# Two-layer hybrid trunk on one core: the first layer's modulation weights in couples, its norm's squares summed on VectorE

## The chip, the cores and the metric

The kernel runs on one core of a Trainium2 chip. The metric is the device time of one execution in microseconds; several executions are timed and their median is given. Engines are called by the profile's names: PE (TensorE's matmuls), PEld (its weight loads), DVE (VectorE), ACT (ScalarE), POOL (GpSimd) and SP (SyncE, which here only issues DMAs).

## The reference, cut to what matters

A trunk of two layers over 256 context tokens and 256 latent tokens of width 1024. Each layer mixes tokens (RWKV-7 heads beside gated linear attention) and then applies a feed-forward part, a dense SwiGLU in the first layer and eight experts in the second. Only the beginning of the first layer matters here:

```python
mod_x = jnp.split((silu_c @ ada_w[i] + ada_b[i])[:, None, :], 6, axis=-1)
mod_c = jnp.split((silu_cc @ ada_w[i] + ada_b[i])[None, None, :], 6, axis=-1)
hx = modulate(rmsnorm(x, norm_mix_pre[i]), mod_x[0], mod_x[1])
hc = modulate(rmsnorm(h_ctx, norm_mix_pre[i]), mod_c[0], mod_c[1])
# rmsnorm(x, g) = x * rsqrt(mean(x * x) + eps) * g;  modulate(h, shift, scale) = h * (1 + scale) + shift
pc, px = hc @ w_in, hx @ w_in
```

So every value of `h` needs the norm over all 1024 features of its token, and its feature's shift (the first sixth of the modulation) and scale (the second sixth). The first projection needs all of `h`.

## The kernel before, in words

Activations lie with features on the 128 partitions: 8 blocks (k = 0 to 7) of 128 features by 512 tokens. Weights stream from memory in pieces of 1 MB (128 partitions by 2048) through a ring of three `raw` buffers; SP issues the loads in the order of the list `pieces` (class `Stream`, line 267), and the load of a piece waits until the matmuls of the piece three places ahead of it have read their buffer. When a piece of the projection is used, it is split in halves: `hi` is a rounded copy made by ACT (line 299) and `lo` the remainder made by DVE (line 300), and each product is three matmuls (`hh` by `hi`, `hl` by `hi`, `hh` by `lo`; line 386), where `hh` and `hl` are the rounded copy and the remainder of `h`.

The order of the work is the order in which the program text issues it: every engine has its own queue of instructions and gets them in that order. Generators interleave the streams; `staggered(gens, lag)` starts one generator every `lag` rounds and steps all live ones once a round.

The modulation of one layer is 24 pieces of 256 outputs each; pieces 0 to 3 are the shift and 4 to 7 the scale of the first norm. One piece is one generator `ada(l, i, i + 1)`: PE multiplies the conditioning by the piece in two steps of eight matmul instructions (line 408), ACT copies the resulting row to SBUF (`arow`, line 412), PE turns the row into columns (line 417), DVE adds the bias and writes `mods` (line 419). After piece 7 one DVE instruction makes `gsc`, the norm's weight times (1 + scale), for all eight blocks (line 427).

`h_first` (line 1713 and on) is the beginning of the first layer. POOL's queue loads the small constants and then the whole input `xc` (2 MB). The pieces 0 to 7 go through `staggered` with a lag of 2, and the generator `stats` stands between the third and the fourth: for each block ACT squares it (line 461) and PE adds the squares over the partitions by a matmul with ones (line 467); ahead of the last squares a tiny Ln makes ACT load its table (line 454). At the end ACT computes `rstd` with Ln and Exp (lines 474 and 475). Then `W.ahead` splits the first projection piece, and `norm_mod` makes the eight blocks: `xn` = input times `rstd` (line 494, DVE or POOL), `h` in two halves of 256 tokens on ACT (line 501), `hh` (line 517 on ACT, line 520 on DVE) and `hl` (line 521, DVE or POOL). Its loop makes block k's `h` ahead of `hh` and `hl` of block k - 1. `mixing` then starts the projection; its first two output blocks run interleaved, 48 matmuls that go through k = 0 to 7.

Of the kernel before, what the change touches and what calls it, by code (L numbers as in the profile page):

```python
# [7 lines left out]
F32 = mybir.dt.float32  # L8
# [8 lines left out]
P = 128  # L17
# [20 lines left out]
         [("rw", b) for b in (14, 12, 13, 8, 9, 10, 11, 4, 0, 5, 1, 6, 2, 7, 3)])  # L38

GLA_QKV, GLA_O, GLA_V = (5, 9), 13, 20  # L40
FGROUPS = [(0, 8), (8, 15), (15, 22)]

FFN_END = 24 + 8 + 14 + 4 + 22 + 24
# [83 lines left out]
def body(tc, nc, A):  # L127
# [10 lines left out]
    def nm(s):  # L138
        cnt[0] += 1
        return f"{s}{cnt[0]}"  # L140
# [52 lines left out]
    def bc(ap, n):  # L193

        return bass.AP(tensor=ap.tensor, offset=ap.offset, ap=[*ap.ap, [0, n]])
# [6 lines left out]
    def run(g):  # L202
        for _ in g:
            pass
# [125 lines left out]
            b = self.take()  # L330
            return (a[0], b[0]), (a[1], b[1])

    for i in range(8):
        pieces.append((A["ada"][0, i], PIECE, False))
    for i in range(14):
        pieces.append((A["win"][0, i], PIECE, True))
# [62 lines left out]
    def ada(l, i0, i1, tag="acc"):  # L399

        for i in range(i0, i1):
            yield tag
            raw = W.get()[0][0]
            pt = ps(tag)
            for kk in range(2):
                for q in range(4):
                    k = 2 * q + kk
                    mm(pt[32 * q:32 * q + 32, :256], silc[:, k, :], raw[:, k * 256:k * 256 + 256],
                       start=(kk == 0), stop=(kk == 1), tile_position=(0, 32 * q))
                yield  # L410
            row = wp.tile([P, 256], F32, tag="arow", name=nm("arow"), bufs=2)
            sc.copy(row, pt[:, :256])
            back(tag)
            yield tag
            pt = ps(tag)
            for b in range(2):
                mm(pt[:, 2 * b:2 * b + 2], row[:, b * P:b * P + P], K("sel"), start=True, stop=True)
            yield
            ve.tensor_tensor(mods[l][:, 2 * i:2 * i + 2, :], pt[:, 0:4].rearrange("p (a b) -> p a b", b=2),
                             bc(V(l, "ada_b", 2 * i, 2 * i + 2), 2), ALU.add)  # L420
            back(tag)
            if i % 4 == 3:
                c = i // 4
                m = mods[l][:, 8 * c:8 * c + 8, :]
                if c in (1, 4):
                    n = V(l, "norm_mix_pre" if c == 1 else "norm_ffn_pre")
                    ve.scalar_tensor_tensor(gsc[l][0 if c == 1 else 2], m, 1.0, bc(n, 2), ALU.add, ALU.mult)
                if c in (2, 5):
                    n = V(l, "norm_mix_post" if c == 2 else "norm_ffn_post")
                    ve.tensor_tensor(gsc[l][1 if c == 2 else 3], m, bc(n, 2), ALU.mult)  # L430
            yield True

    def staggered(gens, lag):

        live, t, todo = [], 0, list(gens)
        while live or todo:
            if todo and t % lag == 0:
                live.append(todo.pop(0))
            live = [g for g in live if steps(g, 1)]
            t += 1  # L440
# [37 lines left out]
    def stats(src, q, out, late):  # L478
        for k in range(KB):
            q.add(src[:, k, :])  # L480
            q.mm()
            yield
        for _ in range(late):
            yield
        out.append(q.r())

    def norm_mod(l, which, res, r, n0, hh, hl, tp, keep=None):

        n = T - n0
        sh = mods[l][:, 24 * which:24 * which + 8, :]  # L490
        g = gsc[l][2 * which]
        def norm(e, k):
            xn = tp.tile([P, T], F32, tag="xn" if e is ve else "pxn", name=nm("xn"), bufs=2)[:, :n]
            e.tensor_tensor(xn, res[:, k, :], r, ALU.mult)
            return xn

        def mod(k, xn):
            h = keep[:, k, :] if keep is not None else tp.tile([P, T], F32, tag="h", name=nm("h"), bufs=NH)[:, :n]
            for (a, b, m) in SEG:
                if a >= n0:  # L500
                    sc.activation(h[:, a - n0:b - n0], xn[:, a - n0:b - n0], AF.Identity, scale=g[:, k, m:m + 1],
                                  bias=sh[:, k, m:m + 1])
            return h
        if hh is None:
            for k in range(KB):
                mod(k, norm(ve, k))
                yield
            return

        hs, xs = {}, {k: norm(gp, k) for k in XN_POOL[:2]}  # L510
        for k in range(KB + 1):
            if k < KB:
                h = hs[k] = mod(k, xs.pop(k) if k in xs else norm(ve, k))
                if k == XN_POOL[0]:
                    xs.update({q: norm(gp, q) for q in XN_POOL[2:]})
                if k in HH_ACT:
                    sc.copy(hh[:, k, :n], h)  # L517
            if k > 0:
                if k - 1 not in HH_ACT:
                    ve.tensor_copy(hh[:, k - 1, :n], hs[k - 1])  # L520
                (gp if k - 1 in HL_POOL else ve).tensor_tensor(hl[:, k - 1, :n], hs[k - 1], hh[:, k - 1, :n], ALU.subtract)  # L521
                yield
# [1187 lines left out]
    with tc.manual_schedule():  # L1710
        banks(**MAIN)

        def h_first(l):
            sp = ExitStack()
            W.sp = sp.enter_context(pool("sp", "right"))
            hs = ExitStack()
            hp = hs.enter_context(pool("hp", "right"))
            hh = hp.tile([P, KB, T], F32R, name="hh0")
            hl = hp.tile([P, KB, T], F32R, name="hl0")
            with pool("ra") as ra:  # L1720
                res = ra.tile([P, KB, T], F32, name="res0")
                gp.dma_start(res, A["xc"])
                r = []
                first = [ada(l, i, i + 1) for i in range(8)]
                staggered(first[:3] + [stats(res, Squares(T, hp, "pa", "xn"), r, 3)] + first[3:], 2)
                W.ahead(W.i, 2)
                run(norm_mod(l, 0, res, r[0], 0, hh, hl, hp))

            def close():
                hs.close()  # L1730
                sp.close()
            return hh, hl, hp, close

        y, og, left = mixing(0, h_first)
        rs = ExitStack()
        rb = rs.enter_context(pool("rb", "right"))
        res = rb.tile([P, KB, T], F32, name="res")
        gp.dma_start(res, A["xc"])
        sp2 = ExitStack()
        W.sp = sp2.enter_context(pool("sp", "right"))  # L1740
        W.nhi = 4
        W.limit = 2 * FFN_END
        st = rb.tile([P, T], F32, name="st0")
        with pool("op", "right") as tp:
            r = out_proj(0, y, og, res, 0, tp, Squares(T, tp))
            ve.tensor_copy(st, r)
        left.close()
        ls = ExitStack()
        res1 = ls.enter_context(pool("ra")).tile([P, KB, T], F32, name="res1")
        with pool("fh", "right") as hp:  # L1750
            nxt = ffn(0, res, st, res1, hp)
        sp2.close()
        rs.close()

        def h_second(l):
            sp = ExitStack()
            W.sp = sp.enter_context(pool("sp", "right"))
            W.nhi = 2
            W.limit = 2 * (FFN_END + 14)
            hs = ExitStack()  # L1760
            hp = hs.enter_context(pool("hp", "right"))
            hh = hp.tile([P, KB, T], F32R, name="hh1")
            hl = hp.tile([P, KB, T], F32R, name="hl1")
            nxt.tp = hp
            W.ahead(W.i, 2)
            run(norm_mod(l, 0, res1, nxt.r(), 0, hh, hl, hp))
            gp.dma_start(A["rx"], res1[:, :, 256:512])
            ls.close()

            def close():  # L1770
                hs.close()
                sp.close()
            return hh, hl, hp, close

        y, og, left = mixing(1, h_second)
        rs = ExitStack()
        rb = rs.enter_context(pool("rb", "right"))
        res = rb.tile([P, KB, 256], F32, name="res")
        gp.dma_start(res, A["rx"])
        sp3 = ExitStack()  # L1780
        W.sp = sp3.enter_context(pool("sp", "right"))
        W.nhi = 4
        W.limit = 1 << 30
        st = rb.tile([P, 256], F32, name="st1")
        with pool("op", "right") as tp:
            r = out_proj(1, y, og, res, 256, tp, Squares(256, tp))
            ve.tensor_copy(st, r)
        left.close()
        xr = ExitStack()
        W.widen(xr.enter_context(pool("xr")), 6)  # L1790
        moe(1, res, st)
        xr.close()
        sp3.close()
        rs.close()
        psum[2].close()
# [85 lines left out]
```

## Time and profile before

| | |
|---|---|
| median of 3 executions | 2387.55 us (2386.76 to 2390.78) |
| the profiled execution's own time | 2388.32 us |
| its span in the profile | 2386.5 us |
| mean granted TensorE clock | 0.939 of full speed |
| PE busy | 2172.3 us (91%) |
| DVE busy | 1517.9 us (64%) |
| ACT busy | 1264.7 us (53%) |

The span is measured from the first to the last record of the profiled execution; its own time is 1.8 us longer. Busy shares are averages over stages with different limits: the change touches only the beginning, so that stretch is read by itself. In the timeline each line gives the start, the duration, the engine, the line of the program and what is written from what; a bracket tells how long the engine had been idle before and which instruction or load ended the wait.

### The profile page before, as it was taken

To read this page: it belongs to the slowest core of one execution; us is meant where nothing else is said; L and a number is where in the kernel's file an instruction comes from. 1 tells how busy PE (TensorE), PEld (TensorE's weight loads), DVE (VectorE), ACT (ScalarE), POOL (GpSimd) and SP (SyncE) were. 2 spreads that over 40 slices of the span, in tenths; PEclk is the share of its full clock that TensorE was granted. 3 is DMA by queue.
4 is the path that set the end of the run, shared out by engine and by line. 5 is a ranking of instruction groups with operands and counts; after the bars stand their busy time and mean duration, and the time that the engine had idled before them with its cause. 6 is when DMAs were issued, how large, how long until landed. Compare 5 with 4: busy or idle time off the path is not lost. (4 is left out here: it accounts for less than half of the span.)

```text
span 2386.5 us, 37180 instructions
## 1 busy us (share of the span) xinstructions
PE 2172.3 (91%) x14845; PEld 1718.9 (72%) x14845; DVE 1517.9 (64%) x2204; ACT 1264.7 (53%) x1861; POOL 240.9 (10%) x597
## 2 busy tenths in 40 slices
PE   6999888978699999879978887699999999999997
PEld 3777666766488888658756776578778787887875
DVE  2547555753532333365765565488998998999996
ACT  4435434544423222354554344577777777777775
POOL 1000034430200000120003451000000000000000
PEclk8989889998799999979986898899999999999998
DMA  6211354323023231212223432469998998999981
GB/s 261 85 66 59 121 179 148 101 89 124 22 76 122 70 127 66 84 67 89 76 97 111 129 106 72 179 261 345 346 351 328 342 362 332 348 346 352 364 346 69
DMA packets 110310, 430.79 MB, mean 181 GB/s; under 512 B 51584, under 2 KB 54144, under 8 KB 62000
## 3 DMA queue, kind: packets, MB, share of 16 engines
q1 hardware_dynamic: 102800, 377.53, 43.7%
q10 hardware_dynamic: 5472, 39.85, 4.8%
q0 software_dynamic: 1856, 10.95, 1.3%
q8 instruction: 118, 1.93, 0.3%
q14 instruction: 64, 0.52, 0.1%
HBM read 417.81 MB, written 10.49 MB: 179 GB/s over the span
## 5 line engine op out<-in xcount | busy, mean ns | idle before, releaser
L300 DVE TENSOR_TENSOR lo<-raw,hi 128x1024 fp32r<-128x1024 f32 (+1 forms) x668 | 797.2, 1222 | 209.1 <-ACT hi L299 196.6
L299 ACT CAST hi<-raw 128x1024 fp32r<-128x1024 f32 (+1 forms) x668 | 685.2, 1048 | 157.3 <-PE ps_acc L1586 68.2
L1586 PE MATMUL ps_acc<-hi,gh 128*128 128x512 f32 x704 | 285.1, 405 | 0.0
L1586 PE MATMUL ps_acc<-hi,gl 128*128 128x512 f32 x704 | 278.6, 396 | 0.0
L1586 PE MATMUL ps_acc<-lo,gh 128*128 128x512 f32 x704 | 278.1, 395 | 0.0
L386 PE MATMUL ps_acc<-hh,hi 128*128 128x512 f32 (+1 forms) x448 | 181.1, 404 | 12.5 <-ACT hh L517 10.6
L386 PE MATMUL ps_acc<-hl,hi 128*128 128x512 f32 (+1 forms) x448 | 172.7, 385 | 2.9 <-POOL hl L521 2.2
L386 PE MATMUL ps_acc<-hh,lo 128*128 128x512 f32 (+1 forms) x448 | 172.5, 385 | 1.5 <-DVE lo L300 1.5
L1586 PEld LDWEIGHTS ps_acc<-lo,gh 128*128 128x128 f32 x704 | 132.3, 188 | 32.1 <-DVE lo L300 0.2
L1586 PEld LDWEIGHTS ps_acc<-hi,gl 128*128 128x128 f32 x704 | 132.6, 188 | 27.0
L1586 PEld LDWEIGHTS ps_acc<-hi,gh 128*128 128x128 f32 x704 | 132.4, 188 | 27.2
L1610 PE MATMUL ps_pc<-hi,eah 128*128 128x512 f32 x352 | 139.6, 397 | 0.0
L1610 PE MATMUL ps_pc<-lo,eah 128*128 128x512 f32 x352 | 139.2, 395 | 0.0
L1610 PE MATMUL ps_pc<-hi,eal 128*128 128x512 f32 x352 | 139.2, 395 | 0.0
L386 PEld LDWEIGHTS ps_acc<-hh,hi 128*128 128x128 f32 x448 | 89.0, 199 | 36.9 <-ACT hh L517 11.6
L1400 DVE TENSOR_TENSOR s<-s,ps_pa 128x512 f32<-128x512 f32 x22 | 15.1, 687 | 141.0 <-PE ps_pa L374 141.0
L386 PEld LDWEIGHTS ps_acc<-hl,hi 128*128 128x128 f32 x448 | 88.8, 198 | 20.0 <-POOL hl L521 3.6
L386 PEld LDWEIGHTS ps_acc<-hh,lo 128*128 128x128 f32 x448 | 88.7, 198 | 18.5 <-DVE lo L300 2.8
L547 POOL TENSOR_TENSOR xn<-macc,rstd 128x256 f32<-128x256 f32 x2 | 1.8, 923 | 853.8 <-ACT rstd L475 853.8
L873 POOL TENSOR_TENSOR Tt<-Nl,Tl 64x15 f32<-64x15 f32 (+7 forms) x240 | 69.5, 290 | 153.2 <-DMA Nl<-nsc 135.8
L467 PE MATMUL ps_pc<-nsq,ones 128*128 128x512 f32 (+1 forms) x112 | 56.9, 636 | 30.2 <-ACT nsq L461 30.1
L374 PE MATMUL ps_acc<-fhh,hi 128*128 128x512 f32 x176 | 69.5, 395 | 10.3 <-ACT fhh L517 10.3
(408 smaller groups left out, 4355.5 us busy)
## 6 DMA issues: line engine op xcount, KB each, us to landing
raw<-moe SPq DMA_DIRECT2D x264, 1024.0 KB, 5.7
raw<-ada ACTq DMA_DIRECT2D x34, 1024.0 KB, 5.1
raw<-win SPq DMA_DIRECT2D x28, 1024.0 KB, 4.9
raw<-fgu SPq DMA_DIRECT2D x22, 1024.0 KB, 4.9
raw<-ada SPq DMA_DIRECT2D x14, 1024.0 KB, 5.1
raw<-fdn SPq DMA_DIRECT2D x16, 448.0 KB, 3.2
res<-xc POOLq DMA_DIRECT2D x2, 2048.0 KB, 12.4
Q<-tsc SPq DMA_DIRECT2D x32, 128.0 KB, 2.8
```

What stands on the lines that cost most here:

```text
L299: sc.copy(hi[:, :n], t[:, a * HALF:a * HALF + n])
L300: ve.tensor_tensor(lo[:, :n], t[:, a * HALF:a * HALF + n], hi[:, :n], ALU.subtract)
L374: mm(out, w[:, o:o + P], x[:, k, n0:n1], start=(n == 0 and j == 0), stop=(n == len(ks) - 1 and j == 2))
L386: mm(out, a[:, o], x[:, k, n0:T], start=(k == 0 and j == 0), stop=(k == KB - 1 and j == 2))
L467: mm(self.pt, ones, self.todo.pop(0)[:, :self.n], start=(self.made == 0), stop=(self.made == KB - 1))
L547: e.tensor_tensor(t, m[:, k, :], r, ALU.mult)
L873: gp.tensor_tensor(tmp[:, u, j], bc(Nl[:, s, t], s + 1), bcm(Tl[:, s, j], NB - 1 - s), ALU.mult)
L1400: ve.tensor_tensor(s, s, pu, ALU.mult)
L1586: mm(pg, x[:, k, :], ww, start=(k == 0 and j == 0), stop=(k == 7 and j == 2))
L1610: mm(pd[q], x[:, i * P:i * P + P], ww, start=(c == 0 and i == 0 and j == 0), stop=(c == 10 and i == 1 and j == 2))
```

## The change

The input is loaded by SP's queue in two halves ahead of all pieces. The eight modulation pieces come in the order of `FIRST`, a piece of the shift followed by the piece of the scale for the same 256 features, and `gsc` is made couple by couple. The squares are summed on DVE into two tiles, so that only those two go through PE. The blocks of `h` are made two at a time by a new `block`, the first two after the seventh piece, the others after the eighth; POOL takes no part, and `hh` is made by ACT for the first four blocks and by DVE for the rest. `W.ahead`, which splits the first projection piece, now stands behind all blocks. `norm_mod` is still used by the second layer.

```diff
+FIRST = (0, 4, 1, 5, 2, 6, 3, 7)
...
-    for i in range(8):
+    for i in FIRST:
         pieces.append((A["ada"][0, i], PIECE, False))
...
-            if i % 4 == 3:
+            if l == 0 and 4 <= i < 8:
+                ve.scalar_tensor_tensor(gsc[l][0][:, 2 * i - 8:2 * i - 6, :], mods[l][:, 2 * i:2 * i + 2, :], 1.0,
+                                        bc(V(l, "norm_mix_pre", 2 * i - 8, 2 * i - 6), 2), ALU.add, ALU.mult)
+            elif i % 4 == 3:
...
-                gp.dma_start(res, A["xc"])
-                r = []
-                first = [ada(l, i, i + 1) for i in range(8)]
-                staggered(first[:3] + [stats(res, Squares(T, hp, "pa", "xn"), r, 3)] + first[3:], 2)
+                for q in range(2):
+                    sy.dma_start(res[:, 4 * q:4 * q + 4], A["xc"][:, 4 * q:4 * q + 4])
+                g, sh = gsc[l][0], mods[l][:, 0:8, :]
+                pt = ps("pa")
+                r = hp.tile([P, T], F32, tag="rstd", name="rstd", bufs=1)
+                sq = [hp.tile([P, T], F32, tag="h", name=nm("acc"), bufs=NH) for _ in range(2)]
+
+                def squares():
+
+                    for k in range(KB):
+                        s = sq[k] if k < 2 else hp.tile([P, T], F32, tag="pxn", name=nm("nsq"), bufs=2)
+                        sc.activation(s, res[:, k, :], AF.Square)
+                        if k > 1:
+                            ve.tensor_tensor(sq[k % 2], sq[k % 2], s, ALU.add)
+                        if k % 2 == 1:
+                            yield
+                    sc.activation(tiny, eps[1e-6], AF.Ln)
+                    yield
+
+                def norm():
+                    for q in range(2):
+                        mm(pt, ones, sq[q], start=(q == 0), stop=(q == 1))
+                    sc.activation(r, pt, AF.Ln, bias=eps[1e-6], scale=1.0 / D)
+                    sc.activation(r, r, AF.Exp, scale=-0.5)
+                    yield
+
+                def block(k):
+                    xn = hp.tile([P, T], F32, tag="xn", name=nm("xn"), bufs=2)
+                    ve.tensor_tensor(xn, res[:, k, :], r, ALU.mult)
+                    h = hp.tile([P, T], F32, tag="h", name=nm("h"), bufs=NH)
+                    for (a, b, m) in SEG:
+                        sc.activation(h[:, a:b], xn[:, a:b], AF.Identity, scale=g[:, k, m:m + 1], bias=sh[:, k, m:m + 1])
+                    (sc.copy if k < 4 else ve.tensor_copy)(hh[:, k, :], h)
+                    ve.tensor_tensor(hl[:, k, :], h, hh[:, k, :], ALU.subtract)
+                    yield
+                first = [ada(l, i, i + 1) for i in FIRST]
+                staggered(first[:3] + [squares()] + first[3:4], 2)
+                staggered([first[4], norm(), first[5]], 1)
+                for a, p in ((6, 0), (7, 2), (None, 4), (None, 6)):
+                    staggered(first[a:a + 1] if a else [], 1)
+                    run(chained(block(p), block(p + 1)))
                 W.ahead(W.i, 2)
-                run(norm_mod(l, 0, res, r[0], 0, hh, hl, hp))
```

## Rows read from the trace of the kernel before

**Rows 1.** Busy time by stretch: length, each engine's busy time, granted clock, DMA share, GB/s

```profile
0.00:64.70 64.70, 42.84 (x224) 23.50 (x224) 18.57 (x42) 24.85 (x43) 12.23 (x16) 0.87 0.67 253
```

**Rows 2.** Timeline of the opening stretch, 11 to 42 us: start, duration, engine, line, operation

```profile
11.37 1.08 PE L408 MATMUL ps_acc<-raw,silc 128*32 128x256 f32 x8 [2.75 <-DMA raw<-ada]
12.38 1.01 PE L417 MATMUL ps_acc<-cst,arow 128*128 128x2 f32 x4
...
14.47 0.37 ACT L412 COPY arow<-ps_acc 128x256 f32<-128x256 f32 x1 [5.42 <-PE ps_acc L408]
...
20.58 3.78 PE L467 MATMUL ps_pa<-nsq,ones 128*128 128x512 f32 x4 [0.29 <-ACT nsq L461]
...
24.40 0.63 ACT L461 ACTIVATE nsq<-res 128x512 f32<-128x512 f32 x1 [1.08 <-PE ps_pa L467]
...
26.46 0.64 PE L408 MATMUL ps_acc<-raw,silc 128*32 128x256 f32 x8
...
27.03 1.13 PE L467 MATMUL ps_pa<-nsq,ones 128*128 128x512 f32 x2
...
29.18 1.28 ACT L454 ACT_TABLE_LOAD   x1
...
30.47 0.20 ACT L454 ACTIVATE tiny<-eps 128x1 f32<-128x1 f32 x1
...
34.84 0.61 PE L417 MATMUL ps_acc<-cst,arow 128*128 128x2 f32 x4
...
36.40 0.69 ACT L474 ACTIVATE rstd<-ps_pa,eps 128x512 f32<-128x512 f32 x1
...
38.41 0.63 ACT L475 ACTIVATE rstd<-rstd 128x512 f32<-128x512 f32 x1
...
41.83 0.16 DVE L419 TENSOR_TENSOR mods<-ps_acc,vec 128x4 f32<-128x4 f32 x1 [1.68 <-PE ps_acc L417]
```

**Rows 3.** DMA: two stretches of the stretch table, and issues with us to landing

```profile
10.00:12.50 2.50, 1.13 (x9) 0.33 (x9) 0.00 (x0) 0.00 (x0) 0.00 (x0) 1.00 1.08 450
...
25.00:27.50 2.50, 2.50 (x13) 0.83 (x12) 0.00 (x0) 1.29 (x3) 0.00 (x0) 1.00 0.07 30
...
res<-xc POOLq DMA_DIRECT2D x1, 2048.0 KB, 16.9
...
raw<-ada SPq DMA_DIRECT2D x1, 1024.0 KB, 4.8
```

**Rows 4.** Timeline of the split and the blocks, 41 to 49 us, ACT and DVE

```profile
41.12 1.99 ACT L299 CAST hi<-raw 128x1024 fp32r<-128x1024 f32 x2 [0.16 <-DMA raw<-win]
...
43.34 1.22 DVE L300 TENSOR_TENSOR lo<-raw,hi 128x1024 fp32r<-128x1024 f32 x1
...
45.20 1.09 ACT L501 ACTIVATE h<-xn,mods,gsc 128x256 f32<-128x256 f32 x2 [2.08 <-DVE xn L494]
46.32 0.62 ACT L517 CAST hh<-h 128x512 fp32r<-128x512 f32 x1
...
46.97 0.69 DVE L521 TENSOR_TENSOR hl<-h,hh 128x512 fp32r<-128x512 f32 x1 [1.21 <-ACT hh L517]
...
47.96 0.43 DVE L520 CAST hh<-h 128x512 fp32r<-128x512 f32 x1 [0.30 <-ACT h L501]
48.31 0.68 DVE L494 TENSOR_TENSOR xn<-res,rstd 128x512 f32<-128x512 f32 x1
```

**Rows 5.** Timeline of PE in the first projection, 46 to 65 us

```profile
46.99 0.80 PE L386 MATMUL ps_acc<-hh,hi 128*128 128x512 f32 x1 [5.19 <-ACT hh L517]
...
52.84 0.63 PE L386 MATMUL ps_acc<-hh,lo 128*128 128x512 f32 x1
...
58.38 0.40 PE L386 MATMUL ps_acc<-hh,hi 128*128 128x512 f32 x1
...
64.32 0.39 PE L386 MATMUL ps_acc<-hh,lo 128*128 128x512 f32 x1
```

**Rows 6.** Busy time by stretch around PE's pause, columns as in group 1

```profile
40.00:42.00 2.00, 1.30 (x12) 0.73 (x10) 0.32 (x2) 1.25 (x2) 1.61 (x2) 0.83 0.85 250
42.00:44.00 2.00, 0.00 (x0) 0.00 (x0) 1.97 (x3) 1.11 (x2) 0.00 (x0) 0.50 0.96 360
```

## The prediction, made before the changed kernel was run

> **What bounds the kernel now.** I read the stretch table first. The first 64.7 us hold everything that the diff touches, and PE is busy for 42.84 of them [rows 1]. Behind that stretch comes a chain through the projection, the scans and the experts in which each stage needs the one before it. Nothing in it is tied to absolute time, because the ring of three weight buffers can't run ahead by more than three pieces, so I take a shift of the first projection's end as a shift of the whole kernel.
>
> Then the timeline, engine by engine. In the opening stretch PE works through eight modulation pieces: two groups of eight matmuls and one turn of the row (`sel`) for each. The eight took 1.08 us at first and 0.64 us later, a turn 1.01 and then 0.61 [rows 2]. That is the lower and the upper of TensorE's two levels (1.2 and 2.4 GHz). The granted clock column reads 1.00 through those early microseconds, so there I go by durations. The squares of the input lie between, each on ACT with two `ones` matmuls behind it: four took 3.78 us at the lower level, two took 1.13 at the upper [rows 2]. ACT waited 1.08 us for PE before one of them, and PE, waiting in turn, freed buffers late: the DMA moved 450 GB/s in the stretch from 10 us and 30 GB/s in that from 25 us [rows 3]. That is the loss that the change can attack.
>
> The last modulation result lands on DVE at 41.83 us [rows 2]. Then two casts on ACT and two subtractions on DVE split the first projection piece [rows 4], and the eight blocks of `hh`/`hl` follow. There the reader is to see the order: while one block is multiplied, the block before it is split, and POOL takes some of the operations. PE starts at 46.99 us, **before** the blocks are complete, and follows them; the last of the first 48 matmuls starts at 64.32 and ends at 64.7 us [rows 5]. In this first stretch the blocks and the projection overlap almost fully. The number to beat is 64.7 us.
>
> **The change, part by part.**
>
> *Loads.* The two halves of `xc` (1 MB each) come ahead of the pieces in SP's queue, which also carries the pieces; POOL's queue loses its 2 MB. The second piece, which is the second 1 MB of that queue before, had landed by 11.4 us [rows 2]; the second half of `xc` takes its place. One more MB at 450 GB/s [rows 3] or a little less is 2.4 us, less some half microsecond that POOL's share of `xc` had cost this queue by then: the first piece lands at about 13.3 us, the next two at 15.8 and 18.2. The input comes earlier than before, where it took 16.9 us from issue [rows 3]. Each later piece waits until its buffer's former matmuls are through, plus 4.8 us for a load alone [rows 3].
>
> *Squares.* Sixteen matmul instructions become four, six additions of 128x512 come to DVE. No such addition is in the rows; the same shape's multiply took 0.68 us [rows 4] and I take 0.69 (at least the 0.43 of a copy, at most the 1.22 of half the split [rows 4]: within 4 us for all six, on DVE, idle here). ACT's row copy of the second piece ends at about 19.3, so two squares, the third piece's copy, then six squares at 0.63 to 0.69 us each end ACT's part at 26.4 us. The table for Ln costs 1.28 plus 0.20 [rows 2], and **the fourth piece's row copy is queued behind it**: 28.2 us, though its matmuls were through at 25.3. On PE the next pieces are queued behind that copy's turn.
>
> *The norm.* PE: turn 0.6, eight matmuls 0.6, two sums 2.1 (from the 1.13 row): 31.6 us. ACT: Ln 0.69, a second table load 1.28, Exp 0.63 [rows 2]: `rstd` at 34.3 us, and the fifth piece's row copy stands behind all three. The last piece's buffer is held by the fifth's second half behind the sums, so it can't land before about 37 us. Then fifth, sixth and seventh pieces follow each other on ACT and PE by 0.37 (copy), 0.6 (turn), 0.6 (second half) and some 0.1 of handing over: 1.7 us each. The seventh's modulation is on DVE at 39.5 us. Against 41.83 for the last one before, this part does win; it wins little because ACT's queue takes PE's old place.
>
> *The blocks.* They are emitted one after another: `xn` on DVE, `h` on ACT, `hh` on ACT (first four) or DVE, `hl` on DVE, and only then the next block's `xn`. DVE takes its instructions in order: at 46.97 it had stood 1.21 us for `hh` [rows 4] although the `xn` of a later block, behind it in its queue, had its inputs. So each block costs the length of its chain: 0.68 + 0.10 + 1.09 + 0.62 + 0.69 = 3.2 us with ACT's `hh`, 0.68 + 0.10 + 1.09 + 0.43 + 0.69 = 3.0 us with DVE's [rows 4], with a few hundredths for each handing over. The two-step overlap of before and POOL's help are gone. Blocks 0 and 1: 39.5 + 6.4 = 45.9. The eighth piece's row copy is behind block 1 on ACT (45.6); turn 0.6, modulation and its new small scale instruction 0.3: 46.6. That part is nearly hidden. Blocks 2 and 3 to 53.0, blocks 4 to 7 (4 x 3.03) to 65.1 us.
>
> *The split of the first projection piece* stands behind the blocks in the code. ACT's casts run beside the last `hl`, DVE's two subtractions don't: 1.22 us to 66.4 us for the first, the second by 67.6 beside PE.
>
> *The first projection* now finds everything made, but starts with all its work ahead. Two matmuls need no `lo`; 46 remain at 66.4. Between the start at 52.84 and that at 58.38 thirteen steps took 0.426 us each (lower level), from there to 64.32 twenty-six took 0.229 (upper) [rows 5]. PE will have had little to do for 20 us, as before it started here (0.00 us busy in the two microseconds from 42, granted clock 0.50) [rows 6], so I give it the same 13 slow steps: 5.6 + 33 x 0.229 = 13.1, end 79.5 us.
>
> **Sum:** 79.5 - 64.7 = +14.8 us. Against the profiled execution (2388.32 us, span 2386.5) that gives 2403.1; that execution stands 0.8 us above the median of 2387.55, so against the median 2402.4 us. The bounds: 46 matmuls all at the upper level end at 76.9 (2.6 less), all at the lower at 86.0 (6.5 more); loads 0.6 us earlier and shorter hand-overs take 1.5 off; PE's share of the pieces and norm at the lower level instead puts 5 on.
>
> *The clock in the pieces.* The granted clock was 0.83 in the two microseconds from 40 and 0.50 in those from 42, after PE had had 1.30 of 2 us to do [rows 6]; while it was kept busier, the durations stayed at the upper level. In the changed kernel PE waits for ACT between 25.3 and 28.3 us and often after. The Trainium skill, page "TensorE: Matmul & The Clock Gate", section "Part 1: The HAM clock gate", says that the half-rate state is the default and that only activity lifts it; by that, PE could be back at half rate from 28 us. My sum takes the upper level there; the other is a rival below.
>
> **The rivals.** 0.2% or 4.8 us is about what a measurement can tell from no change here.
>
> *PE stays at the lower level through the pieces.* Turns and eights cost 1.0 instead of 0.6, the two sums 3.8 instead of 2.1: the seventh modulation comes at 44.4, everything behind 5 us later: about 2407.5. For it: the gaps that ACT's queue puts into PE. Against: PE is busy without a break from about 16 to 25 us. With the projection slow as well it is 2414. This is the rule named above.
>
> *Early start.* If ACT's squares, tables and copies don't hold up the pieces, they land every 2.5 to 3 us and the seventh modulation is made at about 31. The serial blocks then end at 56.6, the first `lo` at 57.8, the projection at 68.3 (upper level) to 70.9: +3.6 to +6.2, 2391 to 2394. Against: the two table loads and three row copies that stand behind the norm in one queue.
>
> *Faster: an engine passes over an instruction that waits.* Place: DVE and ACT. Then `xn` of the next block runs while `h` of this one is made, the row copies don't wait for the norm, blocks cost DVE's own 1.4 to 1.8 us each, and with a start at 31 the last ends at about 47, the split at 48 to 49, the projection at 60.5: -4 us or a little more, 2383. It decides where `xn` of block 1 starts before `hl` of block 0 ends. The 1.21 us row speaks against it.
>
> *The change doesn't do what it says* only in one sense: the couples come, but just the first couple of blocks is made beside a piece; that is in the sum.
>
> **Chances.** The sum as it stands 0.73; the lower level through the pieces 0.16; early start 0.06, split over the bound; passing over 0.04; 0.01 for the rest. Range 2396 to 2410: it takes in the bounds on both sides and the first rival, leaves out the two lighter ends. Faster by over 0.2% 0.04, within 0.2% 0.05, slower 0.91.
>
> **What would show it.** Right: in the new timeline `xn`, `h`, `hh`, `hl` of one block follow each other without the next block's `xn` between them, some 3 us from one `xn` to the next; the fourth piece's row copy behind the Ln table load; the first projection matmul between 63 and 68 us, with `lo` behind the last `hl`; POOL empty of `xn` and `hl`; from then on the old stages shifted by one amount. Wrong: PE's first projection matmul before 55 us, blocks at under 2 us each, or a later stage that gives the shift back.

## The result and the profile after

The changed kernel took 2417.2 us (median of 4 executions, 2410.13 to 2422.58) against 2389.16 us (4 executions, 2386.76 to 2394.96): a ratio of 1.0112, 95% interval 1.0074 to 1.0150. It is slower by some 28 us where 14.8 were forecast, and outside the range that ended at 2410. Over all experiments the changed kernel ran 16 times (mean 2414.8 us, standard error 1.2) and the kernel before beside them 50 times (mean 2391.4, standard error 0.6): 23.4 us, give or take 1.4. Its three series, each against the runs of the kernel before beside it, differ in the mean by 26.8, 24.7 and 20.3 us.

The profiled execution is one of the longer ones (2422.09 us). The page's span and its first lines:

```profile
span 2420.2 us, 37169 instructions
...
PE 2180.3 (90%) x14833; PEld 1725.0 (71%) x14833; DVE 1521.9 (63%) x2216; ACT 1266.7 (52%) x1864; POOL 232.4 (10%) x590
```

Busy times moved little (PE's by 8.0 us, where the span grew by 33.7): most of the time was lost by waiting. Its timeline of the pieces and the norm answers to [rows 2] (start, duration, engine, line, operation):

```profile
14.58 1.94 PE L410 MATMUL ps_acc<-raw,silc 128*32 128x256 f32 x16 [14.58 <-DMA raw<-ada]
...
18.68 1.08 PE L410 MATMUL ps_acc<-raw,silc 128*32 128x256 f32 x8 [2.16 <-DMA raw<-ada]
...
28.95 1.28 ACT L1743 ACT_TABLE_LOAD   x1
...
30.35 0.35 ACT L414 COPY arow<-ps_acc 128x256 f32<-128x256 f32 x1
...
30.76 1.02 PE L419 MATMUL ps_acc<-cst,arow 128*128 128x2 f32 x4 [2.81 <-ACT arow L414]
...
32.71 3.78 PE L1748 MATMUL ps_pa<-acc,ones 128*128 128x512 f32 x4
...
36.43 1.31 PE L410 MATMUL ps_acc<-raw,silc 128*32 128x256 f32 x16
...
36.53 0.69 ACT L1749 ACTIVATE rstd<-ps_pa,eps 128x512 f32<-128x512 f32 x1 [5.83 <-PE ps_pa L1748]
...
39.07 0.35 ACT L414 COPY arow<-ps_acc 128x256 f32<-128x256 f32 x1
...
41.26 1.01 PE L419 MATMUL ps_acc<-cst,arow 128*128 128x2 f32 x4 [0.47 <-ACT arow L414]
...
45.73 0.16 DVE L421 TENSOR_TENSOR mods<-ps_acc,vec 128x4 f32<-128x4 f32 x1 [3.06 <-PE ps_acc L419]
```

The reader sees the two hold-ups that were forecast: the fourth piece's row copy right behind the Ln table, the fifth's behind Ln, the Exp table and Exp. And one that the sum had left to a rival: a turn takes 1.01 or 1.02 us and the two sums 3.78, so PE works at its lower level through most of the pieces.

The blocks, the split and PE's start, answering to [rows 4, 5]:

```profile
45.81 0.69 DVE L1755 TENSOR_TENSOR xn<-res,rstd 128x512 f32<-128x512 f32 x1
...
46.54 1.09 ACT L1758 ACTIVATE h<-xn,mods,gsc 128x256 f32<-128x256 f32 x2 [1.91 <-DVE xn L1755]
47.66 0.62 ACT L1759 CAST hh<-h 128x512 fp32r<-128x512 f32 x1
48.31 0.69 DVE L1760 TENSOR_TENSOR hl<-h,hh 128x512 fp32r<-128x512 f32 x1 [1.81 <-ACT hh L1759]
48.92 0.68 DVE L1755 TENSOR_TENSOR xn<-res,rstd 128x512 f32<-128x512 f32 x1
...
70.40 0.69 DVE L1760 TENSOR_TENSOR hl<-h,hh 128x512 fp32r<-128x512 f32 x1
...
70.90 0.79 PE L388 MATMUL ps_acc<-hh,hi 128*128 128x512 f32 x1 [18.18 <-ACT hi L301]
71.01 2.35 DVE L302 TENSOR_TENSOR lo<-raw,hi 128x1024 fp32r<-128x1024 f32 x2
...
72.29 0.80 PE L388 MATMUL ps_acc<-hh,lo 128*128 128x512 f32 x1 [0.17 <-DVE lo L302]
...
84.11 0.57 ACT L1271 COPY gad<-ps_acc 32x512 f32<-32x512 f32 x1
```

From one `xn` to the next are 3.11 us, with DVE and ACT waiting for each other in turn; PE stands idle for 18.18 us and then has all 48 matmuls before it. ACT's copy of `gad` is the first work behind those 48. Its start is called **the mark** below: 64.80 us before, 84.11 here.

```profile
64.80 0.57 ACT L1266 COPY gad<-ps_acc 32x512 f32<-32x512 f32 x1
```

### The profile page after: what moved, and what is told of

It reads as the page before. It is cut to its first block, busy times and chain, and to the rows that moved or that the text cites. A ratio compares the mean times of both kernels' runs of the same rounds, so it can differ in the third digit from the quotient of the medians.

```text
span 2420.2 us, 37169 instructions
## 1 busy us (share of the span) xinstructions
PE 2180.3 (90%) x14833; PEld 1725.0 (71%) x14833; DVE 1521.9 (63%) x2216; ACT 1266.7 (52%) x1864; POOL 232.4 (10%) x590
## 3 DMA queue, kind: packets, MB, share of 16 engines
q1 hardware_dynamic: 103088, 379.63, 43.5%
## 5 line engine op out<-in xcount | busy, mean ns | idle before, releaser
L388 PEld LDWEIGHTS ps_acc<-hl,hi 128*128 128x128 f32 x448 | 88.1, 197 | 17.2 <-DVE hl L526 1.3
```

What stands on the lines that cost most here:

```text
L388: mm(out, a[:, o], x[:, k, n0:T], start=(k == 0 and j == 0), stop=(k == KB - 1 and j == 2))
```

## The experiments

Theory A: the loss is that of the start-up, some 20 us at the mark, and the rest of the 28 is a spread between executions. Its main rival, B: a late start costs more again behind the mark. The parts of the start-up's loss are then taken apart one by one. Each edit is to the changed kernel unless the text says otherwise.

**The changed kernel again, twice,** unaltered.

> The changed kernel once more, unaltered. Two parts are told apart by the mark, the start of ACT's copy of gad, the first work behind the first projection's 48 matmuls (64.80 us before, 84.11 after). Theory A (only the beginning is changed; what is lost later is TensorE's granted clock falling at other moments of the scans, from run to run and in any kernel): the mark again at 83 to 85, the stretch from the mark to the end anywhere between 2322 and 2336 us, so runs from 2408 to 2423 us. Rival B (the change makes the scans slower by itself): the mark the same and the stretch behind it again near 2336, every run above 2418.

> The changed kernel a third time, for more times and a third profile. Theory A: the mark at 83 to 86; runs between 2405 and 2423 us, the mean of all runs so far (2416) minus that of the kernel before (2390) comes down to the shift of the mark, 20 to 22 us. Rival B (something behind the mark is slower by itself): the difference of the means stays at 24 us or more, and the profile's stretch behind the mark is above 2330.

The marks were 85.68 and 84.41 us, and the stretch behind the mark 2320.0 and 2326.3 us, where the first profile had 2336.1. The first ran 2407.44 to 2421.02 us, the second 2409.41 to 2416.93. So the start-up is lost every time (mean mark of the three profiles 84.73), and what follows varies by 16 us with the same program. The stretch table from the mark to the output projection of the first layer, for the kernel before, the changed kernel's first profile, and its second, in this order (length, busy times, granted clock, DMA share, GB/s):

```profile
64.80:545.40 480.60, 431.52 (x4673) 339.00 (x4673) 285.64 (x554) 215.72 (x380) 95.47 (x277) 0.94 0.33 104
```

```profile
84.10:575.20 491.10, 443.49 (x4673) 347.43 (x4673) 285.19 (x554) 215.83 (x380) 95.13 (x277) 0.91 0.32 102
```

```profile
85.70:567.30 481.60, 432.18 (x4673) 339.68 (x4673) 282.98 (x554) 215.90 (x380) 95.79 (x277) 0.94 0.33 104
```

Same number of instructions, ACT within 0.2 us; PE is busy 12 us longer where the granted clock is 0.91 instead of 0.94, and the stretch is 10 us longer. The changed kernel's second profile has the length of the kernel before. The mark of 85.68 lies just above what was expected, the stretch behind it, 2320.0, below. Runs well under 2418 us and two stretches near those of the kernel before speak against B as it was put. Theory A's number isn't met either: the means differ by 23.4 us (give or take 1.4), not 20 to 22.

**The kernel before again, twice,** as a measure of its own spread.

> The kernel before once more, for a second profile. Theory A (TensorE's clock rises and falls at other moments in every run): its mark anywhere between 60 and 65 us by when the clock rises in the first projection, all work of ACT and DVE ahead of it unmoved (blocks from 44 to 45 us on), and the stretch behind the mark between 2318 and 2332. Rival: 64.8 and 2322 again within 0.5 us.

> The kernel before against itself. Theory A: ratio 1 within 0.3%, the runs spread over 12 us or more, and the profile's mark between 60 and 65 with the stretch behind it between 2318 and 2332. Rival: runs within 3 us of each other, which would make the spread of the changed kernel its own.

Marks 63.87 and 64.54, stretches behind it 2327.3 and 2325.2 us. The second time, in 12 runs, it ran from 2387.96 to 2403.20 us, ratio to itself 0.9997 (0.9981 to 1.0013). So the spread is not the changed kernel's own, and the mean mark of three profiles before is 64.40: the start-up's shift is 84.73 - 64.40 = 20.3 us.

**The kernel before, delayed.** Does lateness alone cost more later?

```diff
                 W.ahead(W.i, 2)
+                for _ in range(29):
+                    d = hp.tile([P, T], F32, tag="xn", name=nm("late"), bufs=2)
+                    ve.tensor_tensor(d, res[:, 0, :], r[0], ALU.mult)
                 run(norm_mod(l, 0, res, r[0], 0, hh, hl, hp))
```

> The kernel before with 29 further multiplies on DVE (0.645 us apart, so 18.7 us) between the split and the blocks; nothing else is moved. Theory A: the mark at 83 to 85 and, behind it, the same spread as in the changed kernel, so 2405 to 2423 us, median about 2412. Rival B: the mark the same, but the stretch behind it as in the kernel before (2320 to 2326 us), so 2405 to 2411 us in every run.

The multiplies took less than I had set (first `h` at 62.44 instead of 45.20: 17.2 us), and the mark came only 14.4 us late, 79.18: PE reached its upper level at 69.5, five microseconds after its start at 64.2, where the kernel before needed eleven ([rows 5]). The stretch behind was 2323.7 us. The runs: 2411.02 us median (2401.11 to 2416.45), ratio 1.0086 (1.0062 to 1.0110), which is 15 to 26 us. Its lower end lies just above the delay of the mark (14.4 us, 14.8 from the mean mark of 64.40): there may be a rest of some us here too, but this doesn't tell A from B.

**Overlapping blocks.**

```diff
-                def block(k):
...
+                def blocks(k0, k1):
+                    hs = {}
+                    for k in range(k0, k1 + 1):
...
+                            ve.tensor_tensor(xn, res[:, k, :], r, ALU.mult)
+                        if k > k0:
+                            (sc.copy if k <= 4 else ve.tensor_copy)(hh[:, k - 1, :], hs[k - 1])
...
+                                sc.activation(h[:, a:b], xn[:, a:b], AF.Identity, scale=g[:, k, m:m + 1], bias=sh[:, k, m:m + 1])
+                        if k > k0:
+                            ve.tensor_tensor(hl[:, k - 1, :], hs[k - 1], hh[:, k - 1, :], ALU.subtract)
+                        yield
...
-                for a, p in ((6, 0), (7, 2), (None, 4), (None, 6)):
-                    staggered(first[a:a + 1] if a else [], 1)
-                    run(chained(block(p), block(p + 1)))
+                staggered(first[6:7], 1)
+                run(blocks(0, 2))
+                staggered(first[7:8], 1)
+                run(blocks(2, 8))
```

> The changed kernel with the blocks in two overlapping steps: the next block's xn ahead of hh and hl of this one, blocks 2 to 7 in one go. Theory (the serial chain of 3.0 to 3.2 us a block is what the blocks cost): blocks cost 1.7 to 1.8 us each, the last hl ends near 63 instead of 71, the mark comes at 76 to 77 instead of 84.1, and the time falls by 8 us. Rival (the blocks are bound by the engines' own work or by something that the trace doesn't show): the mark stays within 2 us of 84.

Its timeline of DVE late in the blocks, and the mark:

```profile
58.36 0.68 DVE L1758 TENSOR_TENSOR xn<-res,rstd 128x512 f32<-128x512 f32 x1
58.96 0.42 DVE L1760 CAST hh<-h 128x512 fp32r<-128x512 f32 x1
...
59.41 0.69 DVE L1766 TENSOR_TENSOR hl<-h,hh 128x512 fp32r<-128x512 f32 x1
60.02 0.68 DVE L1758 TENSOR_TENSOR xn<-res,rstd 128x512 f32<-128x512 f32 x1
...
76.12 0.57 ACT L1271 COPY gad<-ps_acc 32x512 f32<-32x512 f32 x1
```

Late in the blocks DVE works without a pause, 1.66 us a block instead of 2.9 to 3.1; the last `hl` starts at 62.39 instead of 70.40, the mark is at 76.12. Median 2403.58 us, ratio 1.0069 (1.0044 to 1.0095). The serial chain is shown as the blocks' price: 8 of the 20 us.

**An earlier split.**

```diff
                     staggered(first[a:a + 1] if a else [], 1)
+                    if p == 2:
+                        W.ahead(W.i, 2)
                     run(chained(block(p), block(p + 1)))
-                W.ahead(W.i, 2)
```

> The changed kernel with the split of the first projection piece moved ahead of blocks 2 to 7, so that PE can follow the blocks as before; the blocks stay serial. Theory (PE's start behind all blocks costs the length of the 48 matmuls): PE starts at about 54 instead of 71, its blocks end 2.4 us later (73), the mark comes at about 76 instead of 84.1, 8 us less. Rival (PE, following a slow chain, stays at the lower clock level, and the 48 matmuls take the time that the overlap saves): the mark at 82 to 86.

```profile
53.08 2.36 DVE L302 TENSOR_TENSOR lo<-raw,hi 128x1024 fp32r<-128x1024 f32 x2
54.36 0.80 PE L388 MATMUL ps_acc<-hh,lo 128*128 128x512 f32 x1 [0.44 <-DVE lo L302]
...
60.98 0.50 PE L388 MATMUL ps_acc<-hh,hi 128*128 128x512 f32 x1 [0.95 <-ACT hh L1759]
...
74.97 0.57 ACT L1271 COPY gad<-ps_acc 32x512 f32<-32x512 f32 x1
```

Mark 74.97, 2404.61 us median, ratio 1.0067 (1.0041 to 1.0094). PE follows the serial blocks with waits of 0.2 to 1 us and still gains 10 us: where PE starts is worth about as much as the blocks' chain. The two edits were not run together by themselves, so that 8 and 10 add up to the loss is not shown. (The rival's lower level didn't hold: the matmul at 60.98 took 0.50 us, behind a wait.)

**The norm first.** Squares, Ln table and norm are issued ahead of the first piece, blocks as changed.

```diff
-                staggered(first[:3] + [squares()] + first[3:4], 2)
-                staggered([first[4], norm(), first[5]], 1)
+                run(squares())
+                run(norm())
+                staggered(first[:4], 2)
+                staggered(first[4:6], 1)
```

> The changed kernel with all squares, the Ln table and the norm issued ahead of the first modulation piece; the blocks stay serial. Theory (ACT's queue holds the row copies behind the Ln table, Ln, the Exp table and Exp, and so the pieces): rstd is ready at 22 to 26 instead of 39.2 us, no row copy waits behind a table load, the seventh modulation is on DVE at 36 to 42 instead of 45.7, and the mark (start of ACT's copy of gad) comes at 74 to 81 instead of 84 to 86. Rival (PE at its lower level and the ring of buffers set the pieces' pace, not ACT): the seventh modulation at 44 or later, the mark within 2 us of 84.

```profile
13.38 3.77 PE L1748 MATMUL ps_pa<-acc,ones 128*128 128x512 f32 x4 [13.38 <-DVE acc L1740]
...
19.19 0.63 ACT L1750 ACTIVATE rstd<-rstd 128x512 f32<-128x512 f32 x1
19.73 0.35 ACT L414 COPY arow<-ps_acc 128x256 f32<-128x256 f32 x1
...
37.87 0.16 DVE L421 TENSOR_TENSOR mods<-ps_acc,vec 128x4 f32<-128x4 f32 x1 [3.06 <-PE ps_acc L419]
```

`rstd` is there at 19.8 us, half the time of the changed kernel and earlier than the 22 to 26 expected; the seventh modulation comes at 37.9 instead of 45.7, the mark at 76.99 (2402.06 us, one run). The place of the norm in ACT's queue costs 8 us of the pieces. Not all of it is loss against the kernel before: there `rstd` came at 39.04 us too, and the last modulation at 41.83 [rows 2], 3.9 us ahead of the changed kernel's seventh.

**mid and gab held back.** In the profile after, POOL's queue issues these two loads at once, since nothing of POOL's work stands ahead of them any more:

```profile
3.02 0.53 POOL L1182 DMA_DIRECT2D mid<-mid  x1
3.54 0.54 POOL L1183 DMA_DIRECT2D gab<-gab  x1
```

The experiment makes them wait for the last `hl`:

```diff
+        if l == 0:
+            gp.tensor_copy(mid2[:, 0:1], hl[:, 7, 0:1])
         gp.dma_start(mid2, A["mid2"][l])
```

> The changed kernel with the loads of mid and gab (0.8 MB on POOL's queue, at 3.0 us there, at 58.9 in the kernel before) held back behind the last hl. Theory: they take 1.9 us of the loads' time at the start; the first modulation piece is used at 12.7 instead of 14.6 us, and the mark comes 1 to 2 us earlier, 82 to 84. Rival (they fill gaps): the first piece at 14 or later, the mark unchanged.

```profile
13.43 1.93 PE L410 MATMUL ps_acc<-raw,silc 128*32 128x256 f32 x16 [13.43 <-DMA raw<-ada]
...
15.83 1.08 PE L410 MATMUL ps_acc<-raw,silc 128*32 128x256 f32 x8 [0.47 <-DMA raw<-ada]
```

The first piece is used at 13.43 us, 1.15 earlier where this theory had 1.9. The second gains more: 15.83 instead of 18.68, that is 2.85 us, and ACT's squares stand behind its row copy. The mark is at 82.71 (2404.63 us, one run): 1.4 to 3.0 us below the marks of the changed kernel. The Trainium skill, page "Trainium Kernel Development and Optimization", section "Key Constraints", says that transfers issued from SP's, ACT's and POOL's queues share the same sixteen DMA engines and interleave. The 1.15 us of the first piece and the 2.85 of the second agree.

**The input on POOL's queue, as before** (`gp.dma_start(res, A["xc"])` in place of the two loads of SP).

> The changed kernel with the input loaded by POOL's queue as before (one 2 MB load behind the constants). Theory (the input first makes every piece wait, and buys nothing since the squares come behind the second piece's row copy anyway): the first piece is used at 6.7 instead of 14.6 us, the squares end within 1 us of the 29 us of the changed kernel because the input lands at about 20, so the seventh modulation is at 43 to 46 instead of 45.7 and the mark at 82 to 85: nearly nothing, as the norm sets the pace. Rival (the late first piece is carried to the end): the seventh modulation at 38 to 40, the mark at 76 to 79.

The first piece is used at 6.43 us, `rstd` is ready at 34.9, the seventh modulation at 42.1, the mark at 81.42 (2409.50 us, one run). The squares end at 24.8 us, so the theory's 28 to 30 is missed, and the seventh modulation lies between the two: of the 8 us that the first piece gains, 3.3 reach the mark. Loading the input first costs 3 us in this order of work (2.7 to 4.3 against the three marks of the changed kernel), and brings nothing, because the first square stands behind the second piece's row copy (22.05 us in the profile after).

**The squares on PE, as before,** with the pieces in one list:

```diff
-                pt = ps("pa")
...
-                staggered(first[:3] + [squares()] + first[3:4], 2)
-                staggered([first[4], norm(), first[5]], 1)
+                rr = []
+                staggered(first[:3] + [stats(res, Squares(T, hp, "pa", "xn"), rr, 3)] + first[3:6], 2)
+                r = rr[0]
```

> The changed kernel with the sum of the squares on PE as before, eight matmuls of two passes on the way, and the pieces around it in one staggered list; the blocks stay serial. Theory (ACT's queue, not PE's, held the pieces; the sum on DVE gives PE time but the norm's place in ACT's queue takes it back): PE's sums bring it to its upper level by about 27 us, the row copies of the fifth and sixth piece come ahead of Ln and Exp, and the seventh modulation is at 39 to 44, no later than the 45.7 of the changed kernel; the mark at 77 to 84. Rival (the sum on DVE is worth what it takes from PE, some 7 to 11 us): the seventh modulation at 50 or later, the mark at 88 or later.

The seventh modulation at 44.5, just above what was expected, the mark at 83.10 (2414.35 us, one run), 1.6 us below the changed kernel's mean mark, which is as much as its three marks differ. PE's eights take 0.64 us from 31 us on, and the row copies of the fifth and sixth piece come ahead of Ln. The rival is refuted: taken with its place in the order, summing on DVE saved nothing. As the order of the pieces changed too, what the sum on DVE is worth by itself is not shown.

**All of it together**, but for the loads of `mid` and `gab`: squares and norm first, the first piece's turn behind the norm, each couple's blocks in overlapping steps (`blocks` as above) behind its second piece, the split ahead of the last couple.

```diff
-                def block(k):
...
+                def blocks(k0, k1):
...
+                def split():
+                    W.ahead(W.i, 2)
+                    yield
-                staggered(first[:3] + [squares()] + first[3:4], 2)
-                staggered([first[4], norm(), first[5]], 1)
-                for a, p in ((6, 0), (7, 2), (None, 4), (None, 6)):
-                    staggered(first[a:a + 1] if a else [], 1)
-                    run(chained(block(p), block(p + 1)))
-                W.ahead(W.i, 2)
+                run(squares())
+                steps(first[0], 4)
+                run(norm())
+                seq = []
+                for c in range(4):
+                    seq += [first[2 * c], chained(first[2 * c + 1], *([split()] if c == 3 else []), blocks(2 * c, 2 * c + 2))]
+                staggered(seq, 2)
```

> The changed kernel with the squares and the norm first, the first piece's turn behind the norm, every couple's two blocks made in overlapping steps right behind its second piece and beside the next couple's pieces, and the split ahead of the last two blocks. Theory: pieces set the pace (2 to 3 us each from about 17 us), the last modulation at 38 to 45, PE starts at 38 to 46 and the mark comes at 52 to 60, so 5 to 12 us less than the kernel before, 2379 to 2386. Rival (the pieces' chain over PE, ACT and DVE, now shared with the blocks' work on ACT and DVE, slows to over 4 us each): the mark at 64 or later, no gain.

```profile
23.84 1.29 DVE L1758 TENSOR_TENSOR xn<-res,rstd 128x512 f32<-128x512 f32 x2
...
40.81 0.79 PE L388 MATMUL ps_acc<-hh,hi 128*128 128x512 f32 x1
40.91 0.16 DVE L421 TENSOR_TENSOR mods<-ps_acc,vec 128x4 f32<-128x4 f32 x1 [0.66 <-PE ps_acc L419]
...
55.47 0.57 ACT L1271 COPY gad<-ps_acc 32x512 f32<-32x512 f32 x1
```

The first blocks are made at 24 us beside the pieces, PE starts at 40.8, the mark is at 55.47: 9 us ahead of the kernel before. Twelve runs: 2386.39 us median (2375.69 to 2391.14), ratio **0.9975 (0.9957 to 0.9992)**; the median lies just above the 2379 to 2386 expected. So a start-up with couples can beat the kernel before, by a little, once ACT's queue and the blocks are in another order. That order was not tried on the kernel before, so how much of the gain is owed to the couples is not shown.

## Why the prediction was wrong

The sign and the main mechanism were right, the size wasn't. Step by step, in the first profile:

| step | predicted, us | measured, us |
|---|---|---|
| first piece used | 13.3 | 14.6 |
| fourth piece's row copy done | 28.2 | 30.7 |
| two sums done | 31.6 | 36.5 |
| `rstd` ready | 34.3 | 39.2 |
| seventh modulation done | 39.5 | 45.9 |
| first two blocks done | 45.9 | 52.1 |
| last `hl` done | 65.1 | 71.1 |
| first `lo` done | 66.4 | 72.2 |
| first 48 matmuls done | 79.5 | 84.0 |

- **The step that failed most is "PE at the upper level" in the norm and the pieces.** The sum took 0.6 for a turn and 2.1 for the two sums; they took 1.0 (the fifth piece's alone 0.61) and 3.78. The table gives it 2.4 us between row copy and sums (31.6 - 28.2 = 3.4 against 36.5 - 30.7 = 5.8) and 1.5 behind `rstd` (39.5 - 34.3 = 5.2 against 45.9 - 39.2 = 6.7): 3.9 of the 6.4 us by which the seventh modulation came late. This is the rival "PE stays at the lower level through the pieces", which had 16%: its 44.4 us for the seventh modulation were nearest to the 45.9 measured. I gave more weight to PE's unbroken work from 16 to 25 us; in the trace that work stood at 1.08 us an eight all along, up to 31.7. The rule of the Trainium skill that was weighed there ("TensorE: Matmul & The Clock Gate", "Part 1: The HAM clock gate": half rate unless activity lifts it) pointed the right way, as the 1.01 us turn at 41.26 shows: the granted clock of the stretch from 41 to 46 us was 0.50. PE was not back at its lower level from 28 us, though, it had never left it. Why it stayed there from 20 to 26 us, busy for 5.45 of 6 us, no run here shows.

```profile
20.00:26.00 6.00, 5.45 (x36) 3.27 (x35) 0.91 (x4) 2.77 (x6) 0.00 (x0) 1.00 0.97 371
...
41.00:46.00 5.00, 4.19 (x28) 2.65 (x32) 0.59 (x4) 0.58 (x2) 0.00 (x0) 0.50 0.86 279
```

- **The loads failed first: they had a part that the sum did not count.** It had the first piece at 13.3 us and the second at 15.8; they were used at 14.58 and 18.68. It let POOL's queue lose 2 MB; it did not ask what was queued behind them and behind POOL's share of the blocks. `mid` and `gab` moved from 58.9 to 3.0 us. Held back, they left the two pieces at 13.43 and 15.83 us and the fourth row copy's end at 27.85, so the 2.5 us by which that copy was late are theirs: the rest of the 6.4, and 1.4 to 3.0 of the mark's. The seventh modulation was then done at 43.5 us, 4.0 behind the sum's 39.5, which leaves the lower level its 3.9. The half microsecond taken off for POOL's share of `xc` stands in no row and was not tested by itself.
- **The blocks were right**: 3.1 and 2.9 to 3.0 us each, no overlap, the eighth piece's copy behind block 1; 19.2 us from the first two blocks' end to the last `hl`, 19.0 measured. The overlapping version shows that it is the order, not the work.
- **PE's part was over-priced** by 1.3 us: PE reached its upper level after five of the slow matmuls behind the first `lo`, not thirteen (the matmul at 74.56 us took 0.40); in the second profile it was after ten. Where the clock rises differs from run to run: the kernel before took eleven microseconds in the profile that I read and five when delayed.
- **"A shift of the first projection's end is a shift of the whole kernel"** holds in the mean to 3 us, and in a single run not at all. Start-up 20.3 us, all runs 23.4 give or take 1.4. The rest of 3.1 us is about twice its uncertainty, and I can't settle it. The kernel with all of it together shows such a rest as well: its mark came 8.9 us earlier, but its mean is only 6.3 us below that of the kernel before beside it (give or take 1.9). If the rest is real, lateness need not be its cause. The profiles behind the mark give 2327.5 us in the mean for the changed kernel (2320.0 to 2336.1) and 2324.7 for the one before (2321.7 to 2327.3), too few to decide. What one profile shows is where such time sits: in the scans, where the granted clock falls at other moments. The first median of 28 us held two runs of 2422 us, the longest of sixteen.

So the start-up's 20.3 us against the 14.8 forecast are the lower level and the loads, less what PE gave back (1.3 us in the first profile); the 28 us of the first comparison hold the open rest and the spread besides. The range failed for both reasons: its top, 2410, left out the lower level together with the spread of 15 us that both kernels show. Three runs of the kernel before, 4 us apart, had hidden that spread.

## What to carry to other kernels

This start-up was set by the order within each engine's queue as much as by its loads: in one like it, put what depends on the early load (here squares, tables and norm) at the head of ACT's queue, not where the text happens to have it, and issue a block's next step ahead of the waiting one, or each block costs its whole latency. When work leaves a queue, look at what stood behind it: here it started at once and delayed other loads. Don't take PE's upper clock level for granted between waits: here the lower one held for most of the first 46 us. And give the range the spread of many runs rather than of three.

## What the runs showed of the hardware that I had not expected

- The same program, run again, differs by 15 us of 2415 (2407.44 to 2422.58), and 9.5 of the 16 us between two of its profiles behind the mark (491.10 against 481.60) lie in one stretch where the granted clock was 0.91 in one and 0.94 in the other.
- PE at 5.45 us busy of 6, from 20 to 26 us, still did its eights in 1.08 us; the step to about 0.65 (two eights in 1.31) came only behind the two sums, at 36.4 us, and was gone again in the turn at 41.26. The granted clock column shows 1.00 for the stretch from 20 to 26 us; durations are the safer reading there.
- 0.85 MB on another queue delayed the first piece's load by 1.15 us and the second's by 2.85; alone, at the 450 GB/s of [rows 3], they would take 1.9 (an estimate).
